# A one-core hybrid block: two unread products in the opening, gate Silus, rotary keys and column sums issued later

## The chip, the core and the metric

The kernel runs on one core of a Trainium2 chip. Its metric is the device time of one execution in microseconds (us), lower is better. The core has five engines with a queue each: TensorE (PE in the profile, with its weight loads as PEld), VectorE (DVE), ScalarE (ACT), GpSimd (POOL) and SyncE (SP, which only issues transfers here). Each engine takes its instructions in the order in which the program was laid out for it, and waits on semaphores for the others.

## The reference, cut to what matters

One layer of a streaming encoder on 512 tokens of width 1024, all in float32. The three parts read and add to the same `x`:

```python
mod = silu(c) @ w_ada + b_ada                  # nine vectors of 1024
h = rms(x) * (1 + s1) + sh1
x = x + 0.5 * g1 * swiglu(h, ffn1_w_in, ffn1_w_out)
h = rms(x) * (1 + s2) + sh2
x = x + g2 * hybrid_mixer(h)                   # two groups of four heads, then w_out
h = rms(x) * (1 + s3) + sh3
x = x + 0.5 * g3 * swiglu(h, ffn2_w_in, ffn2_w_out)
```

The mixer multiplies `h` by `w_in` and splits the result. Group A is a gated delta rule: convolutions and Silu on q, k and v, a chunked recurrence, then `rms(o) * silu(z)` with a gate `z` of its own. Group B is latent attention: low-rank q and kv lifted by two small matrices, norms of each head, rotary positions on 64 columns of every q head and on one key `kr` that all heads share, block-causal softmax, a norm of each head's output. Both groups are put side by side and multiplied by `w_out`.

## The kernel before

Activations stand with features on the 128 partitions and tokens along the row: `xT` is eight tiles of 128x512. A float32 product is written as three products of a reduced type: weights and activations are each split in a high part (a cast on ACT, `wh`, `hh`, `ah`, `mh`) and a low part (a subtraction on DVE, `wl`, `hl`, `al`, `ml`), and `mm3` issues high x high, high x low and low x high (lines 267 to 269). Small products (transposes against the identity, attention, the delta rule) stay in plain float32.

**Stages.** `phase0` (0 to about 62 us) transposes the tokens, works out the first modulation and the first six products of FFN1 while weights stream in. FFN1 goes on to about 330 us, its second matrix (`down`) to about 403 us, the mixer from there to about 692 us, and FFN2 to the end.

**What sets the order.** `phase0` and the body of FFN2 are laid out by hand: under `in_order` every instruction follows the one written before it on its engine. `down`, `first_units` and the delta recurrence keep only their products in written order. The rest of the mixer is written as generators (`Side`) that are stepped by turns between groups of large products; a scheduler then fixes one order for each engine. An activation from another table than the one loaded makes ACT load a table (`ACT_TABLE_LOAD`, 1.28 us); the method `table` therefore chains all Exp and Silu activations in the order in which they are written, through `self.tabled`.

The places that the change touches:

- **Opening** (`phase0`, lines 313 to 330). TensorE turns the token tiles `xt` (line 316). ACT sums their squares (line 321), POOL takes a power for the norm (line 179), DVE scales the first 128 columns (`xn`, line 348). TensorE then makes the columns of the modulation from `ar`, a slice of `w_ada` (line 415), turns `xn` (line 357), sums four partial rows (line 335), turns the last token tile, and waits for the first high part `hh` (line 362, ACT) to make six products of it (line 375); line 442 spreads the norm over the partitions.
- **Column sums at the seams** (`norm_half`, `first_units`). The token norm at the end of a part is worked out by halves. While the first products of the next part run on half 0, `first_units` steps the norm of half 1 at numbered marks: the first step is the column sum (`colsum`, line 536, which needs DVE's or POOL's last addition to `na`, line 478) with what follows it on POOL and DVE (the power and the diagonal `dg`), the second spreads it (line 442), the third modulates. The marks stand at line 735 for FFN2 (`(7, 18, 15)`, the products of two units by turns) and at line 1246 for the mixer (`(6, 15, 14)`, one unit).
- **Rotary key** (`prep_k`, lines 1843 to 1881). The key after its rotation is `kro` (DVE, lines 1889 to 1893 and 1859); four transposes (line 1869) and a copy (line 1871) make `krT`, which each attention block reads at line 1908. Behind it the step goes on with the other key columns, `kn`: squares, a power in nine steps on DVE, a scaling by head, transposes and a scaled copy `nT` (`head_tiles`, lines 1783 and 1785).
- **Gate Silus** (`mixer`, line 2048). When the last of four large gate products is laid out, four Silus of `z` are issued. The attention blocks (`attend`) of the second pair of heads still run then: their Exp, transposes (line 1925), value products (line 1935), copies out (`ao`, line 1948; `hn`, line 1939), and at the end `attended`, which scales (`on`), turns (line 1966) and splits (`mh`, line 1971; `ml`, line 1972) a head. Beside them four inversions of 128x128 blocks run (`inverse`, lines 1573 to 1616, `join`, lines 1636 to 1646). The gate is read only in `gated_out` (line 1760).

Of the kernel before, what the change touches and what calls it, by code (L numbers as in the profile page):

```python
# [14 lines left out]
AF = mybir.ActivationFunctionType  # L15
# [3 lines left out]
P = 128  # L19
# [3 lines left out]
NB = NT // P  # L23
# [56 lines left out]
class Block:  # L80
# [216 lines left out]
    def phase0(self):  # L297

        nc = self.nc
# [13 lines left out]
        def raw(b, j):  # L313
            pt = self.aux()
            for t in range(4):
                nc.tensor.transpose(pt[:, t * P:(t + 1) * P], self.xtok[b][j][:, t * P:(t + 1) * P], self.ident)
            nc.vector.tensor_copy(xall[:, 4 * j:4 * j + 4, b * P:(b + 1) * P], pt.rearrange("p (t c) -> p t c", t=4))
# [8 lines left out]
        r = self.rms_cols(v, NB, D)  # L326
        for i in (4, 5, 6):
            raw(*tiles[i])
        self.c1, self.c2 = self.const([P, KT], s="sh"), self.const([P, KT], s="s1")
        self.new_h()  # L330

# [23 lines left out]
        pt = self.aux()  # L355
# [376 lines left out]

    def ffn2(self, nb):
        with self.tc.tile_pool(name="ws", bufs=1) as self.ws:
            ps = self.first_units(3, nb, 2, (7, 18, 15))
            with self.in_order():
                self.ffn2_rest(ps)

# [500 lines left out]
    def latents(self, nb):  # L1239

        nc = self.nc
        wq = self.up_weight("mla_w_uq", self.vcol["mla_q_norm_w"], 3, 384)
        wkv = self.up_weight("mla_w_ukv", self.vcol["mla_kv_norm_w"], 2, 512)
        next(wq)
        next(wkv)
        ps = self.first_units(3, nb, 1, (6, 15, 14))

        def gather(ps):
            parts, acc = [], None
            for p in ps:  # L1250
                parts.append(self.split(p, "lat"))
                sq = self.slot(s="lsq")
                nc.scalar.activation(sq, p, AF.Square)
                if acc is None:
                    acc = sq
                else:
                    nc.vector.tensor_tensor(out=acc, in0=acc, in1=sq, op=ALU.add)
            return parts, acc

        pk = self.proj(self.aux())  # L1260
        qp, acc = gather(ps)
        ps = [pk]
        lq = qp, self.rms_cols(self.colsum(acc), NB, 384)
        p = self.proj()
        s = self.slot(s="kab")
        nc.scalar.copy(s[:72, :], p[:72, :])
        wq = next(wq)
        ps.append(self.proj())
        kp, acc = gather(ps)
        lkv = kp, self.rms_cols(self.colsum(acc), NB, 256)  # L1270
        wkv = next(wkv)
        return lq, wq, lkv, wkv, s
# [569 lines left out]
    def prep_k(self, kn):  # L1842

        nc = self.nc
        sk_n = self.const([P, 16], s="skn")
        kr = self.kab[:, :288].rearrange("p (b c) -> p b c", b=NB)[:, :, :64]
        s = self.slot(s="krq")
        sv = s[:, :256].rearrange("p (b c) -> p b c", b=NB)
        nc.scalar.activation(sv, kr, AF.Square)
        ss = self.small(4, "krs")  # L1850
        nc.vector.tensor_reduce(out=ss, in_=sv, axis=AX.X, op=ALU.add)
        rr = self.rms_cols(ss, 4, 64)
        kx = self.slot(s="krx")
        xv = kx[:, :256].rearrange("p (b c) -> p b c", b=NB)
        self.mul(xv, kr, self.bc(rr, 4, 64))
        ko = self.slot(s="kro")
        ov = ko.rearrange("p (b e c) -> p b e c", b=NB, e=2)
        self.rope(ov[:, :, 0, :], xv, self.rope_c["k"], self.rope_s["k"])
        nc.vector.tensor_copy(ov[:, :, 1, :], ov[:, :, 0, :])
        yield  # L1860
        for b in range(NB):
            s = self.slot(s="akk")
            nc.scalar.activation(s, kn[b], AF.Square)
            nc.vector.tensor_reduce(out=sk_n[:, 4 * b:4 * b + 4], in_=s.rearrange("p (h d) -> p h d", h=4), axis=AX.X,
                                    op=ALU.add)
        rkn = self.rms_cols(sk_n, 16, 128)
        pt = self.aux()
        for b in range(NB):
            nc.tensor.transpose(pt[:, b * P:(b + 1) * P], ko[:, b * P:(b + 1) * P], self.ident)
        self.krT = self.slot(s="krT")  # L1870
        nc.scalar.copy(self.krT, pt)
        yield
        for b in range(NB):
            kv = kn[b].rearrange("p (h d) -> p h d", h=4)
            self.mul(kv, kv, self.bc(rkn[:, 4 * b:4 * b + 4], 4))
        yield
        jk = self.vcol["qkn_k_nope"]
        for h in range(4):
            self.knT.append(self.head_tiles([kn[b][:, h * P:(h + 1) * P] for b in range(NB)], self.cwT[:, jk:jk + 1]))
            yield  # L1880

    def rope(self, out, x, c, s):
# [76 lines left out]
    def attended(self, h, r):  # L1959


        nc = self.nc
        on = self.head_scale(self.ao[h], r)
        pt = self.aux()
        for i in range(NB):
            nc.tensor.transpose(pt[:, i * P:(i + 1) * P], on[:, i * P:(i + 1) * P], self.ident)
        yield
        j = self.vcol["mla_out_norm_w"]
        gain = self.cwT[:, j:j + 1]
        mh, ml = self.mixed[4 + h] = self.slot(F32R, "mh"), self.slot(F32R, "ml")  # L1970
        nc.scalar.activation(mh, pt, AF.Copy, scale=gain)
        nc.vector.scalar_tensor_tensor(out=ml, in0=pt, scalar=gain, in1=mh.bitcast(F32), op0=ALU.mult, op1=ALU.subtract)


    def mixer(self, nb):
        nc, tc = self.nc, self.tc
# [19 lines left out]
        def silu(tiles):  # L1996
            for t in tiles:
                self.table(t, t, AF.Silu)
# [46 lines left out]

        chain.add(solving())
        self.dense_units(4, Rates(sides, (1, 0.75, 2)), 1, z_done)
        silu(self.zT)
        accum = self.slot(s="na")

        fill = Side()
# [1 line left out]
        def others():  # L2053
            while att.open or att.todo:
                att.step()
                yield
            fill.add(self.out_attended())

        rest = Side(wide=3)
        rest.add(others())  # L2060
        while self.wk[1] is None or deltas.open or deltas.todo:
            chain.step(2)
# [112 lines left out]
```

## Time and profile before

| | us |
|---|---|
| median of 3 runs | 1050.69 |
| the 3 runs | 1050.64, 1050.69, 1052.29 |
| the profiled execution, its own time | 1052.1 |
| its span in the profile | 1050.4 |
| PE busy | 1032.6 |
| DVE busy | 682.1 |
| ACT busy | 449.0 |
| POOL busy | 48.2 |

The span is the stretch that the profile's clock covers; the execution's own time has 1.7 us around it. Lines of the profile name an engine, a line of the kernel, an operation and its tiles as out<-in. In the order of time, a row gives start, length, engine, line, and in square brackets how long the engine was idle before and what released it. In the chain that ended last, a row gives start, share of the chain, engine and line. A row of waits gives the total, the count and the longest. A row of stretches gives the busy time of each engine with the number of instructions, the granted share of TensorE's clock (PEclk) and what the DMA engines did.

### The profile page before, as it was taken

What the parts mean: (1) busy time and instruction counts of PE and PEld (TensorE: products, weight loads), DVE (VectorE), ACT (ScalarE), POOL (GpSimd) and SP (SyncE); (2) the same over time, 40 slices, a digit from 0 to 9 for tenths busy, and PEclk for the clock granted to TensorE, in tenths of its full rate; (3) what the DMA queues carried; (4) which work ended last, traced back from release to release, by engine and by line L of the source; (5) the groups of instructions that cost most, each with busy time, mean ns of one, the idle gap of its engine ahead of it and who ended that gap; (6) DMA issues with size and microseconds to landing.
All of it is one profiled execution on the core that took longest, in us unless ns stands there. A gap on an engine that the chain in (4) does not pass through costs nothing.

```text
span 1050.4 us, 16101 instructions
## 1 busy us (share of the span) xinstructions
PE 1032.6 (98%) x6375; PEld 884.5 (84%) x6375; DVE 682.1 (65%) x1251; ACT 449.0 (43%) x781; POOL 48.2 (5%) x113
## 2 busy tenths in 40 slices
PE   6999999999999999999999999999999999999998
PEld 5788878788887799887777769998999999999986
DVE  4478984333486636648877556789768778777633
ACT  3342322222222226739566464465345444444422
POOL 1000000000000011100001111310000000000000
PEclk8999999999999999999999999999999999999999
DMA  9979973233586539711212201173423333333222
GB/s 275 288 224 301 303 237 101 85 96 95 184 279 220 164 99 236 179 41 51 70 42 55 72 22 41 41 162 100 136 78 102 108 101 112 92 98 105 76 61 81
DMA packets 203689, 136.88 MB, mean 130 GB/s; under 512 B 13777, under 2 KB 186590, under 8 KB 203614
## 3 DMA queue, kind: packets, MB, share of 16 engines
q1 hardware_dynamic: 202318, 131.14, 42.4%
q0 software_dynamic: 1296, 4.72, 2.4%
q8 instruction: 50, 0.82, 0.3%
q14 instruction: 25, 0.20, 0.1%
HBM read 128.63 MB, written 2.49 MB: 125 GB/s over the span
## 4 chain that ended last, share of the span: by engine, by line
PE 89%; ACT 4%; DVE 3%; DMA 1%; issue 1%; POOL 0%; SPq 0%; POOLq 0%; DVEq 0%; ACTq 0%
PE pa L267 20%; PE pa L268 20%; PE pa L269 19%; PE pb L870 6%; PE pb L869 6%; PE pb L871 6%; PE pb L268 1%; PE pb L267 1%; PE pb L269 1%; PE pb L415 1%; PE pb L1491 1%; PE pb L1905 1%; DMA xt<-in_x 1%; PE pb L1908 1%; PE pb L1935 0%
## 5 line engine op out<-in xcount | busy, mean ns | idle before, releaser
L267 PE MATMUL pa<-hh,wh 128*128 128x512 f32 (+1 forms) x565 | 216.7, 384 | 0.0
L268 PE MATMUL pa<-hl,wh 128*128 128x512 f32 (+1 forms) x565 | 214.8, 380 | 0.6 <-DVE hl L454 0.4
L269 PE MATMUL pa<-hh,wl 128*128 128x512 f32 (+1 forms) x565 | 214.6, 380 | 0.0
L193 ACT CAST wh<-wr 128x1024 fp32r<-128x1024 f32 (+1 forms) x106 | 107.8, 1018 | 247.7 <-PE pa L268 172.0
L198 DVE TENSOR_TENSOR wl<-wr,wh 128x1024 fp32r<-128x1024 f32 (+1 forms) x97 | 114.2, 1178 | 104.6 <-ACT wh L193 102.2
L267 PE MATMUL pa<-ah,wh 128*128 128x512 f32 (+1 forms) x396 | 145.6, 368 | 0.6 <-DVE xT L896 0.4
L268 PE MATMUL pa<-al,wh 128*128 128x512 f32 (+1 forms) x396 | 144.5, 365 | 0.0
L269 PE MATMUL pa<-ah,wl 128*128 128x512 f32 (+1 forms) x396 | 143.6, 363 | 0.0
L267 PEld LDWEIGHTS pa<-hh,wh 128*128 128x128 f32 x565 | 106.4, 188 | 23.1 <-issue 3.2
L269 PEld LDWEIGHTS pa<-hh,wl 128*128 128x128 f32 x565 | 106.3, 188 | 20.5 <-issue 0.9
L268 PEld LDWEIGHTS pa<-hl,wh 128*128 128x128 f32 x565 | 106.5, 188 | 19.4 <-DVE hl L454 1.0
L269 PEld LDWEIGHTS pa<-ah,wl 128*128 128x128 f32 x396 | 74.8, 189 | 12.1
L267 PEld LDWEIGHTS pa<-ah,wh 128*128 128x128 f32 x396 | 75.2, 190 | 10.3 <-ACT wh L193 1.7
L268 PEld LDWEIGHTS pa<-al,wh 128*128 128x128 f32 x396 | 75.2, 190 | 7.2
L574 DVE SCALAR_TENSOR_TENSOR aa<-ar,sc,aa 128x512 f32<-128x512 f32 x98 | 72.9, 747 | 9.5 <-DMA ar<-in_w_ada 8.3
L896 DVE SCALAR_TENSOR_TENSOR xT<-pa,mod,xT 128x512 f32<-128x512 f32 (+1 forms) x40 | 29.3, 735 | 17.6 <-PE pa L269 17.6
L869 PE MATMUL pb<-fh,wh 128*128 128x256 f32 x144 | 40.7, 283 | 0.0
L871 PE MATMUL pb<-fh,wl 128*128 128x256 f32 x144 | 40.7, 283 | 0.0
L871 PE MATMUL pb<-hh,wl 128*128 128x256 f32 x144 | 40.7, 283 | 0.0
L870 PE MATMUL pb<-fl,wh 128*128 128x256 f32 x144 | 40.7, 282 | 0.0
L870 PE MATMUL pb<-hl,wh 128*128 128x256 f32 x144 | 40.7, 282 | 0.0
L869 PE MATMUL pb<-hh,wh 128*128 128x256 f32 x144 | 40.6, 282 | 0.0
(443 smaller groups left out, 2008.4 us busy)
## 6 DMA issues: line engine op xcount, KB each, us to landing
wr<-in_ffn_w_in SPq DMA_DIRECT2D x82, 512.0 KB, 3.9
ar<-in_w_ada SPq DMA_DIRECT2D x48, 512.0 KB, 6.0
wr<-in_ffn_w_out SPq DMA_DIRECT2D x34, 512.0 KB, 3.7
ar<-in_w_ada SPq DMA_DIRECT2D x48, 256.0 KB, 4.9
wr<-in_w_in SPq DMA_DIRECT2D x21, 512.0 KB, 3.7
wr<-in_ffn_w_out SPq DMA_DIRECT2D x17, 384.0 KB, 3.4
wl<-wr POOLq DMA_DIRECT2D x9, 512.0 KB, 6.0
wr<-in_w_out SPq DMA_DIRECT2D x8, 512.0 KB, 3.7
```

The lines of the kernel that those rows point to most:

```text
L193: self.nc.scalar.copy(hi, raw)
L198: self.nc.vector.tensor_tensor(out=lo, in0=raw, in1=hi.bitcast(F32), op=ALU.subtract)
L267: mm(out, wh, xh, start=start, stop=False)
L268: mm(out, wh, xl, start=False, stop=False)
L269: mm(out, wl, xh, start=False, stop=stop)
L415: nc.tensor.matmul(pg[32 * q:32 * q + 32, :256], self.sc[:, kc:kc + 1].to_broadcast([P, 32]), a[:, kc], start=(e == 0), stop=(e == 1), til ...
L574: nc.vector.scalar_tensor_tensor(out=acc, in0=a, scalar=sc, in1=acc, op0=ALU.mult, op1=ALU.add)
L869: mm(out, wh, xh, start=start and k == 0, stop=False, **kw)
L870: mm(out, wh, xl, start=False, stop=False, **kw)
L871: mm(out, wl, xh, start=False, stop=stop and k == 3, **kw)
L896: nc.vector.scalar_tensor_tensor(out=self.xT[t][:, ts], in0=p[:, ts], scalar=gate[:, t:t + 1], in1=self.xT[t][:, ts], op0=ALU.mult, op1=AL ...
L1491: nc.tensor.matmul(pa[:, ps], kh[:, ps], x[:, ps], start=True, stop=True)
```

## The change

- In `phase0`, behind the transposes of seven token tiles, TensorE makes the same float32 product of the identity and a token tile twice, into a PSUM tile that nothing reads.
- The first mark of `first_units` goes from 7 to 8 for FFN2 and from 6 to 7 for the mixer.
- The transposes of the rotary key and the copy `krT` go from ahead of the scaling of `kn` to behind the second of four `head_tiles`.
- The Silus of the gate go from the end of the gate's products to the end of the attention blocks; the chain of table activations is first moved on to the last `mh` (`self.ended`), so that the Silus stay behind it on ACT.

```diff
@@ phase0
         for i in (4, 5, 6):
             raw(*tiles[i])
+        unread = self.aux()
+        for _ in range(2):
+            nc.tensor.matmul(unread, self.ident, self.xtok[0][0], start=True, stop=True)
         self.c1, self.c2 = self.const([P, KT], s="sh"), self.const([P, KT], s="s1")
@@ ffn2
-            ps = self.first_units(3, nb, 2, (7, 18, 15))
+            ps = self.first_units(3, nb, 2, (8, 18, 15))
@@ latents
-        ps = self.first_units(3, nb, 1, (6, 15, 14))
+        ps = self.first_units(3, nb, 1, (7, 15, 14))
@@ prep_k
         rkn = self.rms_cols(sk_n, 16, 128)
-        pt = self.aux()
-        for b in range(NB):
-            nc.tensor.transpose(pt[:, b * P:(b + 1) * P], ko[:, b * P:(b + 1) * P], self.ident)
-        self.krT = self.slot(s="krT")
-        nc.scalar.copy(self.krT, pt)
         yield
...
             self.knT.append(self.head_tiles([kn[b][:, h * P:(h + 1) * P] for b in range(NB)], self.cwT[:, jk:jk + 1]))
+            if h == 1:
+                pt = self.aux()
+                for b in range(NB):
+                    nc.tensor.transpose(pt[:, b * P:(b + 1) * P], ko[:, b * P:(b + 1) * P], self.ident)
+                self.krT = self.slot(s="krT")
+                nc.scalar.copy(self.krT, pt)
             yield
@@ attended
-        nc.scalar.activation(mh, pt, AF.Copy, scale=gain)
+        self.ended = nc.scalar.activation(mh, pt, AF.Copy, scale=gain).ins.name
@@ mixer
         self.dense_units(4, Rates(sides, (1, 0.75, 2)), 1, z_done)
-        silu(self.zT)
         accum = self.slot(s="na")
...
                 att.step()
                 yield
+            self.tabled = self.ended
+            silu(self.zT)
             fill.add(self.out_attended())
```

**TensorE in the opening.** Ahead of the modulation's columns stood the last transposes of token tiles (`xt`; `ident` is the identity, `sg` the partial rows, `xn` the scaled first columns). Before:

```order
L316 MATMUL pb_182<-ident_92,xt_81 128x128 x4
L316 MATMUL pb_188<-ident_92,xt_82 128x128 x4
L415 MATMUL pb_222<-ar_108,sc_124 32x256 x8
L357 MATMUL pb_234<-ident_92,xn_212 128x128 x4
L335 MATMUL pb_222<-sel_128,sg_231 128x1 x2
```

With the change:

```order
L316 MATMUL pb_182<-ident_92,xt_81 128x128 x4
L316 MATMUL pb_188<-ident_92,xt_82 128x128 x4
L331 MATMUL pb_194<-xt_76,ident_92 128x512 x2
L418 MATMUL pb_225<-ar_108,sc_124 32x256 x8
L360 MATMUL pb_237<-ident_92,xn_215 128x128 x4
L338 MATMUL pb_225<-sel_128,sg_234 128x1 x2
```

The two unread products stand between the transposes and the columns; nothing else moves there.

**TensorE in the mixer, at the rotary key.** Among the large products for the convolutions (`pa`, from `hh` and `hl` and the split weights `wh`, `wl`) the four transposes of the key `kro` stood alone. Before:

```order
L267 MATMUL pa_4531<-hh_3172,wh_4380 128x512
L1869 MATMUL pb_4461<-ident_92,kro_4426 128x128 x4
L268 MATMUL pa_4531<-hl_3173,wh_4380 128x512
L269 MATMUL pa_4531<-hh_3172,wl_4381 128x512
L267 MATMUL pa_4641<-hh_3158,wh_4526 128x512
```

With the change:

```order
L267 MATMUL pa_4866<-hh_3163,wh_4739 128x512
L1786 MATMUL pb_4502<-ident_92,kn_4042 128x128
L1786 MATMUL pb_4509<-ident_92,kn_4042 128x128
L1881 MATMUL pb_4516<-ident_92,kro_4429 128x128 x3
L1786 MATMUL pb_4502<-ident_92,kn_4043 128x128
L1786 MATMUL pb_4509<-ident_92,kn_4043 128x128
L1881 MATMUL pb_4516<-ident_92,kro_4429 128x128
```

The transposes of `kro` moved behind some fifty more large products, into the run of the sixteen transposes of `kn`, which had stood together at nearly the same place before.

**ScalarE at the end of attention.** Rows with `z` and L168 are the gate's Silus; `ao`, `hn` and `mh` belong to the last heads of attention, `U`, `ti` and `T` to the inversions, whose products TensorE makes between large ones. Before:

```order
L1929 COPY pT_5580<-pb_5575 128x512
L168 ACT_TABLE_LOAD
L168 ACTIVATE z_5288<-z_5288 128x512
L1948 COPY ao_5086<-pb_5582 128x128
L1586 COPY U_5613<-ti_5391 32x4x32 x2
L1598 COPY ti_5244<-pb_5638 32x128 x2
L1988 COPY z_5748<-pa_5679 128x512
L168 ACTIVATE z_5490<-z_5490 128x512
L1939 ACTIVATE hn_5623<-pb_5582 128x256
L1948 COPY ao_5088<-pb_5582 128x128
L168 ACTIVATE z_5671<-z_5671 128x512
L168 ACTIVATE z_5748<-z_5748 128x512
```

With the change the copies of the last heads follow `pT` at once, and behind the last `mh` there stands:

```order
L1975 ACTIVATE mh_5670<-pb_5661,cwT_811 128x512
L1601 COPY ti_5343<-pb_5706 32x128 x2
L1601 COPY ti_5394<-pb_5723 32x128 x2
L168 ACT_TABLE_LOAD
L168 ACTIVATE z_5291<-z_5291 128x512
L168 ACTIVATE z_5493<-z_5493 128x512
L168 ACTIVATE z_5674<-z_5674 128x512
L168 ACTIVATE z_5751<-z_5751 128x512
L1619 COPY T_5802<-pb_5801 64x256
```

The table load and the four Silus moved from ahead of `ao` and `hn` to a place between the last `ti` and the first copy `T` of the inversions. The number of table loads in the program is the same.

On TensorE the laying out of this stretch changed with it: the eight value products (L1935) of the last pair come ahead of the inversions' next products, and of the ten large products that stood right ahead of the last transposes of `on` (L1966) eight others (`pa` from `hh`, for the gate) stand there now, the ten behind. The column sums (L536) at both seams stand three large products later than before. VectorE and GpSimd take a few neighbouring instructions of these stretches in another order; SyncE's order is the same.

## The prediction

> **What bounds the kernel now.** I read the page first: how busy TensorE is, its clock by slices, and the shares of the chain that ended last.
>
> ```profile
> PE 1032.6 (98%) x6375; PEld 884.5 (84%) x6375; DVE 682.1 (65%) x1251; ACT 449.0 (43%) x781; POOL 48.2 (5%) x113
> PEclk8999999999999999999999999999999999999999
> PE 89%; ACT 4%; DVE 3%; DMA 1%; issue 1%; POOL 0%; SPq 0%; POOLq 0%; DVEq 0%; ACTq 0%
> ```
>
> The reader is to see that TensorE is the bound nearly everywhere, and that one slice alone, the first, has less than the full clock. The change takes no product away and adds two. It can save time only where TensorE waits or runs slowly. So I looked next at TensorE's waits, the longest first.
>
> ```profile
> PE pb L305 <- DMA vecs<-in_b_ada: 3.0, 1, 3.0
> PE pb L316 <- DMA xt<-in_x: 2.9, 1, 2.9
> PE pb L415 <- DVE xn L348: 1.9, 1, 1.9
> PE pb L1966 <- DVE on L1229: 1.5, 1, 1.5
> PE pb L1869 <- DVE kro L1859: 0.8, 1, 0.8
> ...
> PE pb L536 <- DVE na L478: 0.5, 2, 0.3
> ```
>
> The first two rows are the start's transfers, which the change leaves alone. The four others are its four places: 4.7 us together. Then I cut the opening into stretches at the moments where the granted clock changes, and set two stretches of the mixer beside them, which hold the 1.5 us wait.
>
> ```profile
> core 0: us, PE busy (x) PEld busy (x) DVE busy (x) ACT busy (x) POOL busy (x), PEclk, DMA share, GB/s
> 12.33:15.74 3.41, 1.46 (x19) 0.83 (x19) 2.89 (x11) 0.12 (x1) 0.73 (x1) 1.00 1.16 316
> 15.74:19.16 3.42, 3.14 (x14) 2.59 (x13) 2.35 (x6) 1.79 (x3) 0.14 (x5) 0.50 1.17 310
> 19.16:22.57 3.41, 3.41 (x7) 1.71 (x6) 1.27 (x2) 0.00 (x0) 0.98 (x30) 0.50 1.21 297
> 22.57:25.98 3.41, 3.41 (x29) 2.38 (x29) 0.54 (x3) 0.96 (x2) 0.00 (x0) 1.00 1.16 314
> ...
> 613.06:616.47 3.41, 2.74 (x14) 1.96 (x13) 0.58 (x2) 3.35 (x9) 0.70 (x1) 1.00 0.00 0
> 616.47:619.88 3.41, 2.55 (x60) 2.10 (x60) 3.09 (x4) 2.11 (x6) 0.00 (x0) 1.00 0.02 5
> ```
>
> This is the view that decides. The clock is 1.00 from 12.33, falls to 0.50 at 15.74, and comes back at 22.57: two stretches of 3.41 us at half pace. The stretch ahead of the fall had TensorE busy for 1.46 of 3.41 us (43%). The two mixer stretches had it busy for 80% and 75%, and the clock stayed.
>
> **The change part by part.** The sum is made against the profiled execution's own time, 1052.1 us.
>
> *The unread products.* Where they go and what they could spare:
>
> ```profile
> 6.30 6.20 PE L316 MATMUL pb<-ident,xt 128*128 128x128 f32 x28 [2.91 <-DMA xt<-in_x]
> ...
> 15.54 0.86 PE pb L357 x4
> ...
> 17.43 0.82 ACT hh L362
> 18.29 1.65 PE pa L375 x3
> 19.94 1.28 PE pb L375 x3
> 21.22 1.59 PE pb L442 x2
> ...
> 602.09 1.72 PE pb L1905 x4
> ```
>
> (The first row is from the order of time, the others from the chain that ended last.) The transposes end at 6.30 + 6.20 = 12.50, and line 415 waits 1.9 us more. Two float32 products of 128x512 at full clock cost 1.72 us: the last row holds two such products, written as four passes. They fit into the pause, so in themselves they cost nothing: xn on DVE hides them. Without that cover, or at half clock (line 442: 1.59 us for one such product, so 3.2 us), up to 1.3 us would come on the path.
>
> With them the stretch from 12.33 has TensorE busy for 1.46 + 1.72 = 3.18 of 3.41 us, 93%, above the 75% at which the clock stayed. If it stays here too, the chain's work between 15.74 and 22.57 runs at full pace: of line 357 0.66 us lie behind 15.74 (it ends at 16.40), line 375 has 1.65 + 1.28, line 442 has 22.57 - 21.22 = 1.35, together 4.94 us, of which half goes: 2.47. Line 335, beside these, halves too. I take **-2.5**. The bounds: 2.9 if line 335's half (it releases hh through a vector operation) comes on top; and 0 if the clock falls all the same. Transfers may take some of it: the DMA share in these stretches is above 1, so the queues are full, and weights needed 2.5 us sooner don't land sooner. I count up to 0.4 for it in the range.
>
> *Column sums.* At the seam into the mixer and at the one into FFN2:
>
> ```profile
> 405.67 0.14 issue
> 405.81 0.57 PE pb L536 x4
> ...
> 694.32 0.61 PE L536 MATMUL pb<-ones,na 128*128 128x1 f32 x4 [0.33 <-DVE na L478]
> ...
> 695.58 0.39 PE L268 MATMUL pa<-hl,wh 128*128 128x256 f32 x1 [0.42 <-DVE hl L454]
> ```
>
> The first two rows are of the chain, the last two of the order of time. Three products of 128x256 (each shorter than the 0.39 us of such a row) now stand ahead of each sum, about as much as the waits. In the mixer's seam the wait goes: the waits' row gives both as 0.5, so 0.17 beside FFN2's 0.33, with 0.14 of issue: **-0.3**. In FFN2 TensorE waits 0.42 us for hl soon after. What it no longer waits for at line 536 it waits for there, because the vector and scalar chain to hl isn't shortened: **0**. The other end for both: -0.6; and +0.4 if the norm of half 1, which now starts three products later, becomes late.
>
> *Rotary key.* The rows in the order of time:
>
> ```profile
> 508.51 0.63 PE L1869 MATMUL pb<-ident,kro 128*128 128x128 f32 x4 [0.79 <-DVE kro L1859]
> ...
> 520.00 2.50 DVE L1229 TENSOR_TENSOR kn<-kn,ry 128x512 f32<-128x512 f32 x4
> ...
> 523.17 2.42 ACT L1785 ACTIVATE nT<-pb,cwT 128x512 f32<-128x512 f32 x4 [1.21 <-PE pb L1783]
> ...
> 524.33 0.48 PE L1908 MATMUL pb<-krT,qrT 64*128 64x128 f32 x2
> ```
>
> The idle 0.79 us goes, since kro is 12 us old where the transposes stand now. The transposes themselves cost the same there. The copy krT now queues on ACT among the four copies nT (2.42 / 4 = 0.6 us each), which end only at 525.6, while line 1908 reads krT from 524.33. It stands behind the second nT, so it lands at about 523.17 + 3 x 0.6 = 525.0, but the transposes of kn also come out earlier by the 0.79 us: late by nearly nothing. What is late next is kn itself (520.00), which VectorE sets; TensorE has large products until then. I take **-0.8**, between -1.1 (switches between small and large products saved too) and 0 (all of it met again at line 1908, since the two later nT now wait 0.6 us behind krT).
>
> *Gate Silus.* Again in the order of time:
>
> ```profile
> 610.19 1.28 ACT L168 ACT_TABLE_LOAD   x1
> 611.49 0.63 ACT L168 ACTIVATE z<-z 128x512 f32<-128x512 f32 x1
> ...
> 614.61 0.36 ACT L1939 ACTIVATE hn<-pb 128x256 f32<-128x256 f32 x1
> ...
> 616.50 1.29 DVE L1229 TENSOR_TENSOR on<-ao,roots 128x512 f32<-128x512 f32 x2 [0.88 <-POOL roots L179]
> 617.33 0.63 PE L1966 MATMUL pb<-ident,on 128*128 128x128 f32 x4 [1.53 <-DVE on L1229]
> ...
> 622.46 0.37 ACT L1616 COPY T<-pb 64x256 f32<-64x256 f32 x1 [1.07 <-PE pb L1615]
> ...
> 625.33 0.79 PE L1636 MATMUL pb<-T,at 64*64 64x64 f32 x10
> ```
>
> Table load and Silus, 1.28 + 4 x 0.63 = 3.8 us, stand ahead of hn, and hn leads through a power on POOL to on, for which TensorE waits 1.53 us. Before, TensorE could turn on 617.33 - 614.61 = 2.7 us after hn began. In the new order hn needs only the value products, which end near 610.9, and two copies U ahead of it: it begins near 611.3, so line 1966 can start near 614.0. TensorE gets there near 613.3, since eight large products still lie ahead of it, and the ten that covered it before lie behind. That leaves some 0.7 us of wait at line 1966 and 0.2 at line 1935, which now reads pT right behind its copy: 1.53 - 0.9 = **-0.6**. Bounds: -1.5 (no new wait) and 0 (the same wait as before). What is queued behind the Silus now is the copies T. The Silus start behind the last ti; in the new order TensorE has fifteen large products and 4 us of small ones between there and line 1636, against some 5 us on ACT for ti, Silus and T. That hides them; without the cover the first T would be late by up to 3.8 us.
>
> The sum: 1052.1 - 2.5 - 0.3 - 0.8 - 0.6 = **1047.9 us**. The median before is 1.4 us below the profiled execution. If the unprofiled runs lost less to the clock in the opening, part of the 2.5 us isn't there to be won, and 1047.9 stands as the floor that both have; if the 1.4 lie elsewhere, the median falls to 1046.5.
>
> **The rivals.**
>
> *The mixer gives its gains back* (line 1908 waits for krT, line 1966 for on). For it: both places end in chains of scalar and vector work that the change reorders but hardly shortens. Against it: TensorE is 89% of the chain, so these chains seldom end last. Time: 1052.1 - 2.5 - 0.3 = 1049.3.
>
> *The clock falls all the same.* In the stretch 15.74 to 19.16 TensorE waits for hh in any case; at full pace its 3.14 us shrink, while the products of line 375 move in, and I estimate 2.4 of 3.42 us busy, 70%, just under the 75% seen to be kept. If that drops the clock at 19.16, one stretch of half pace stays and half of 3.41 us is lost again: 1052.1 - 0.8 - 1.7 = 1049.6. If it falls at 15.74 as now, the opening gives nothing: 1052.1 - 1.7 = 1050.4. For it: at 92% busy (3.14 of 3.42) the half clock was kept at 19.16, so busy time alone doesn't explain the grant. Against it: 43% against 93% is a wide step. The Trainium skill, "TensorE: Matmul & The Clock Gate" (Part 1: The HAM clock gate), has the clock fall only after about 3.4 us of idleness; a pause of 1.9 us would then not be the cause, and the sum would be 1050.4. The row 12.33 to 15.74 speaks against that: 1.46 us of work in it, and the clock fell. Its Part 4 (PE-mode transpose) says that transposes don't count as busy in the same way; no row here shows that apart, and it would favour a later fall, as there are transposes in the stretch from 15.74.
>
> *Slower.* The copies T come late: they stand behind 3.8 us of table and Silus on ACT. If the last ti, which waits for TensorE's small products, comes so late that 2 us of this are uncovered, TensorE idles for 2 us at line 1636, more than the 1.9 us ahead of the clock's fall in the opening, and then two stretches at half pace cost up to 3.4 us more: 1052.1 - 3.6 + 2 + 3.4 = 1053.9. It decides from about 1.7 us of uncovered wait (half of a stretch). Against it: my count above leaves ACT 1 us or more to spare.
>
> **How the numbers follow.** Chances: the forecast 0.50, the mixer's gains given back 0.21, the clock falls all the same 0.22, slower 0.07. A measurement of this kernel tells 0.2% (2.1 us) from no change: faster is below 1048.6, slower above 1052.8. The forecast lies below that bound but for its upper edge, which the two lesser rivals reach down to if the unprofiled 1.4 us count: faster 0.53, same 0.40, slower 0.07. The range: 1045.8 (the median's 1046.5 with the larger opening or key) to 1050.5 (the unchanged clock's 1050.4).
>
> **What would show it.** Right: the granted clock 1.00 in all stretches from 12.33 on, the products inside the pause with line 415 still near 14.45, line 375's six products in about 1.5 us, line 415's second round near 20.2; no wait at line 536 in the mixer's seam and none at the transposes of kro, and at most 0.9 us around lines 1935 and 1966. Wrong: 0.50 in any stretch before 25; a wait for krT at line 1908, for T at line 1636, or for ar at line 415.

## The result, and the profile after

The changed kernel takes 1047.53 us in the median (1047.19 to 1048.07, 6 runs), the kernel before 1051.5 us (1050.64 to 1052.29, 6 runs): a ratio of 0.9967, 95% interval 0.9956 to 0.9978. The profiled execution took 1047.25 us, with a span of 1045.6 us against 1050.4. On another chip, as run e10_after below, the medians were 1047.78 us (12 runs) and 1051.29 us (29 runs), a ratio of 0.9956 (0.9938 to 0.9973).

The page of the changed kernel: engine time and TensorE's clock.

```profile
PE 1029.0 (98%) x6379; PEld 882.2 (84%) x6379; DVE 682.6 (65%) x1251; ACT 448.6 (43%) x781; POOL 48.2 (5%) x113
...
PEclk9999999999999999999999999999999999999999
```

There are four more matmul records (the two unread products, two passes each), and still 3.6 us less of TensorE time: 2.4 us less up to the products that stood at 60 us, where work ran at half clock before, and 0.9 us less in the mixer from 500 to 700 us. The first slice now has the full clock.

TensorE's waits in the changed kernel, total, count and longest:

```profile
PE pb L418 <- DVE xn L351: 1.4, 1, 1.4
PE pb L1939 <- ACT ao L1952: 0.9, 2, 0.4
PE pa L378 <- ACT hh L365: 0.8, 1, 0.8
...
PE pa L267 <- ACT hh L465: 0.4, 1, 0.4
...
PE pb L1786 <- DVE kn L1232: 0.4, 1, 0.4
...
PE pb L1970 <- DVE on L1232: 0.4, 1, 0.4
...
PE pa L268 <- DVE hl L457: 0.3, 1, 0.3
```

The waits for kro and na are gone, and that for on fell from 1.5 to 0.4. New ones stand beside them: for kn 0.4, a second one of 0.4 for the copies of attention, and for hh 0.4 at the seam into FFN2; in the opening the wait for hh at line 378 is 0.8 where it was 0.3, since TensorE arrives sooner at full clock. Each edit passed a part of its wait on.

The opening in stretches of the granted clock (stretch, its length, TensorE busy with the number of instructions, granted clock, then the DMA), and the products in order of time:

```profile
9.71:13.12 3.41, 3.41 (x20) 1.00 1.17 318
13.12:16.54 3.42, 2.03 (x25) 1.00 1.16 315
16.54:19.95 3.41, 2.66 (x14) 1.00 1.16 315
19.95:23.36 3.41, 3.41 (x28) 1.00 1.16 298
...
11.26 1.88 PE L331 MATMUL pb<-xt,ident 128*128 128x512 f32 x4
14.53 1.09 PE L418 MATMUL pb<-ar,sc 128*32 128x256 f32 x16 [1.39 <-DVE xn L351]
17.98 0.96 PE L378 MATMUL pa<-hh,wh 128*128 128x512 f32 x3 [0.75 <-ACT hh L365]
18.78 0.85 PE L378 MATMUL pb<-hh,wh 128*128 128x512 f32 x3
...
20.42 1.09 PE L418 MATMUL pb<-ar,sc 128*32 128x256 f32 x16
```

The unread products lie in the pause, line 418 (415 before) still starts near 14.5, and the clock stays at 1.00.

To see where the 4.8 us of span went, I matched TensorE's instructions of the two traces by code line and tiles and took the difference of their starts:

| place | start, after minus before (us) |
|---|---|
| second round of modulation columns, 22.7 us | -2.3 |
| after 58 us | -2.1 |
| after the seam into the mixer, 406 us | -2.5 |
| last scores of attention, 604 us (2332 large products done in both) | -4.5 |
| first output product of the delta rule, 665 us (2433 done in both) | -4.8 |
| end of the FFN2 products | -4.9 |

So between these places the trace gained 2.1 us (opening), 0.35 (column sums), 2.0 (key) and 0.3 (end of attention). The kernels below show which of this holds in every execution.

### The profile page after: what moved, and what is told of

The parts are those of the page before. It is cut to its first block, busy times and chain, and to the rows that moved or that the text cites. A ratio compares the mean times of both kernels' runs of the same rounds, so it can differ in the third digit from the quotient of the medians.

```text
span 1045.6 us, 16109 instructions
## 1 busy us (share of the span) xinstructions
PE 1029.0 (98%) x6379; PEld 882.2 (84%) x6379; DVE 682.6 (65%) x1251; ACT 448.6 (43%) x781; POOL 48.2 (5%) x113
## 4 chain that ended last, share of the span: by engine, by line
PE 90%; ACT 4%; DVE 4%; issue 1%; DMA 1%; POOL 0%; SPq 0%; POOLq 0%; ACTq 0%; DVEq 0%
PE pa L267 20%; PE pa L268 20%; PE pa L269 20%; PE pb L872 6%; PE pb L873 6%; PE pb L874 6%; PE pb L267 1%; PE pb L268 1%; PE pb L269 1%; PE pb L1909 1%; PE pb L418 1%; PE pb L1939 1%; PE pb L1494 1%; DVE cv L1438 1%; PE pb L1912 1%
```

## The experiments

Beside the time, each execution lists the mean granted clock. That turned out to be the key to these runs: two half-clock stretches of 3.41 us cost 3.41 / 1050, so they show as 0.997, and a single one as 0.998. (Behind the last products of the program the clock falls as well; in the traces that takes up to 0.001 off. An execution with 0.999 or more thus had no other fall.)

**Each edit alone.** e1_products puts only this into the kernel before:

```diff
+        unread = self.aux()
+        for _ in range(2):
+            nc.tensor.matmul(unread, self.ident, self.xtok[0][0], start=True, stop=True)
```

> The kernel before with the two unread products alone. Theory A (the pause lets the clock fall, the products keep it): the granted clock is 1.00 in every stretch from 12.3 us on, the second round of modulation columns starts near 20.4 us instead of 22.7, and the time is 2.0 to 2.4 us below the kernel before. Rival B (the clock in the opening depends on where the free-running stretches fall, not on the products): the clock still falls to 0.50 in some profile, and the time is within 0.5 us of the kernel before. Rival C (they help, but weights land later than needed): 20.4 us as in A, but less than 1.5 us is left at 60 us.

Measured: 1050.22 us (11 runs) against 1051.12 (31 runs), ratio 0.9994 (0.9980 to 1.0008). In the two profiles the second round of columns starts 2.4 us earlier, as A says, but the executions tell more. Of the kernel before, 89 executions in three jobs list their clock: 44 at 0.999 or more, median 1050.24 us, and 45 below, median 1052.35. With the products, ten of eleven show 0.999 or more, median 1050.14; the eleventh shows 0.991 at 1057.9. The products thus remove the fall of the clock, which half of the executions of the kernel before have, and give nothing to the other half. Rival B is right in so far that chance decides, A in that the products take the chance away.

C's number holds too, though weights are not the cause: by 58 us, 1.2 of the 2.4 us are lost again. VectorE in order of time, in the kernel before:

```profile
53.89 0.15 DVE L337 SCALAR_TENSOR_TENSOR s<-pb,vT 128x1 f32<-128x1 f32 x1
53.96 0.16 DVE L1363 COPY ex<-vb 128x4 f32<-128x4 f32 x1
54.08 0.75 DVE L460 SCALAR_TENSOR_TENSOR hm<-xT,s,rb 128x512 f32<-128x512 f32 x1
```

and in e1_products:

```profile
51.53 0.15 DVE L340 SCALAR_TENSOR_TENSOR s<-pb,vT 128x1 f32<-128x1 f32 x1
54.06 0.17 DVE L1366 COPY ex<-vb 128x4 f32<-128x4 f32 x1 [2.38 <-DMA vb<-in_gdn_a_log]
54.14 0.75 DVE L463 SCALAR_TENSOR_TENSOR hm<-xT,s,rb 128x512 f32<-128x512 f32 x1
```

A copy of four columns that is read in the mixer's gates, at 460 us, was scheduled here. In e1_products its vector has not landed, VectorE stands for 2.38 us, and behind it waits hm, on which the next products of FFN1 hang: TensorE then waits 0.56 us for hh and 0.28 for hl. In the kernel before this copy ran at 53.96 us and nobody waited.

e2_key moves only the transposes of the rotary key and their copy, as the change does.

> The kernel before with the rotary key's transposes and copy moved, nothing else. Theory A (the move pays twice: 0.5 us at the key's transposes and some 1.4 us between 548 and 570 us, where the attention of the first heads is ordered in another way): 1.6 to 2.1 us below the kernel before. Rival (only the wait for the key goes; the gain after 548 us belongs to the Silus' move): 0.3 to 0.8 us below.

Measured: 1048.26 us (7 runs), ratio 0.9970 (0.9958 to 0.9981); the four executions at 0.999 or more have a median of 1047.92, against 1050.48 for the 15 such executions of the kernel before in the same job: 2.6 us less. By the traces, at the last scores of attention (2332 large products done in both), it starts 1.10 us earlier though its opening was 0.35 later: 1.45 us. The rival is out. Of theory A's 1.6 to 2.1 us the traces give a little less and the executions more; why they differ by 1.1 us is open (four executions are few, and each of the two traces is of one execution). Theory A's places do not hold. In e2_key three more large products are done by 541 us, 3 x 0.23 = 0.7 us, so the start there, 0.2 us earlier, hides that nearly all of the gain is made by then: 0.2 + 0.35 + 0.7 = 1.2. What seemed a gain after 548 us was those products having moved ahead. TensorE in order of time, before:

```profile
507.32 0.39 PE L267 MATMUL pa<-hh,wh 128*128 128x512 f32 x1
508.51 0.63 PE L1869 MATMUL pb<-ident,kro 128*128 128x128 f32 x4 [0.79 <-DVE kro L1859]
508.89 0.47 PE L268 MATMUL pa<-hl,wh 128*128 128x512 f32 x1
```

and in e2_key:

```profile
520.71 0.44 PE L1783 MATMUL pb<-ident,kn 128*128 128x128 f32 x2 [0.42 <-DVE kn L1229]
520.98 0.49 PE L1878 MATMUL pb<-ident,kro 128*128 128x128 f32 x3
521.31 0.43 PE L1783 MATMUL pb<-ident,kn 128*128 128x128 f32 x2
521.58 0.27 PE L1878 MATMUL pb<-ident,kro 128*128 128x128 f32 x1
521.69 1.59 PE L1783 MATMUL pb<-ident,kn 128*128 128x128 f32 x12
```

Standing alone, the four transposes took 508.89 - 507.32 - 0.23 = 1.34 us of TensorE's time, of which 0.79 was the wait. Within the run they take 0.33 + 0.11 = 0.44 (by the starts). That is 0.9; the other 0.3 and the 0.25 up to 604 us lie in other groupings and in a wait of 0.15 us that went, against 0.42 of new wait for kn. They were not taken apart.

e3_silus moves only the gate's Silus.

> The kernel before with the gate's Silus moved to the end of attention, nothing else. Theory A: TensorE's wait of 1.5 us ahead of line 1966's transposes shrinks to 0.4, a wait of 0.4 for the copies pT or ao appears, and 0.3 to 0.6 us are left at the end. Rival (the gain between 548 and 570 us belongs to this move): 1.6 to 2.0 us below the kernel before. Second rival (the first inversions' copies T are late): no gain.

Measured: 1050.28 us (11 runs), ratio 0.9993 (0.9984 to 1.0003): the median can't tell it. Its profiled execution kept the clock without products, so only differences within the mixer count: -1.52 us up to 566 us, -1.30 at 568, -1.35 at the last scores, -1.64 at 665 us. The end of attention gains 0.3, but 0.2 were lost ahead of it, and 0.1 is left. TensorE's waits in e3_silus:

```profile
PE pb L1935 <- ACT ao L1948: 0.9, 2, 0.4
...
PE pb L1966 <- DVE on L1229: 0.4, 1, 0.4
...
PE pb L1966 <- DVE bt L1546: 0.3, 1, 0.3
```

The wait for on shrank by 1.1, a second one of 0.4 appeared at line 1935: 0.7 fewer, of which 0.3 arrive. The wait for bt is new; it stands at 566 us, ahead of the first heads' transposes at line 1966, and takes the 0.2. T is never waited for. The waits are theory A's; what is left at the end, 0.1 us in this trace, is below its 0.3 to 0.6.

e4_marks moves only the two marks.

> The kernel before with the two first marks moved by one product unit (8 for 7 and 7 for 6), nothing else. Theory A: 0.35 us below, all of it at 404 us, none at 694 us. Rival (the wait moves to the later products there too): 0.0 us.

Measured: 1050.75 us (12 runs), ratio 0.9993 (0.9975 to 1.0011), again too little for the median. (The executions at 0.999 or more have medians of 1049.71 in e3_silus, of seven, and 1049.70 in e4_marks, of six, against 1050.48: 0.8 us less in both, more than the traces show, but within the spread of so few.) In the trace, its lag of 0.39 us from the opening is 0.02 after 406 us: a gain of 0.37, which is theory A. At 694 us nothing changes, as the wait takes another place. TensorE in order of time, e4_marks:

```profile
694.37 0.38 PE L267 MATMUL pa<-hh,wh 128*128 128x256 f32 x1 [0.38 <-ACT hh L462]
...
695.10 0.39 PE L268 MATMUL pa<-hl,wh 128*128 128x256 f32 x1 [0.34 <-DVE hl L454]
...
695.44 0.50 PE L536 MATMUL pb<-ones,na 128*128 128x1 f32 x4
```

**What keeps the clock.** e5_no_products takes the products out of the changed kernel.

> The changed kernel without the two unread products. Theory A (the products only keep the clock from falling, which it does in about half of the executions): the executions in which the mean granted clock stays at 0.999 or more take as long as the changed kernel, about 1047.5 us; others, some half of them, show 0.995 to 0.998 and take 1 to 3 us more; the median is 0.5 to 1.5 us above the changed kernel. Rival (the products pay 2.3 us in every execution, as the two profiles say): all executions about 1049.8 us.

Measured: 1049.31 us (11 runs, 1047.28 to 1052.17). Four executions show 0.999 or more, median 1048.15, seven less, median 1050.27. This is theory A. (Not each of the seven need have lost the clock in the pause: the one that was profiled lost it at 58 us, as shown below.) e6_transposes, on the same chip, has transposes in their place:

```diff
-        for _ in range(2):
-            nc.tensor.matmul(unread, self.ident, self.xtok[0][0], start=True, stop=True)
+        for k in range(14):
+            nc.tensor.transpose(unread[:, k % 4 * P:k % 4 * P + P], self.xtok[0][0][:, k % 4 * P:k % 4 * P + P], self.ident)
```

> The changed kernel with fourteen more unread 128x128 transposes of the same token tile in place of the two unread products, about as long (14 x 0.13 = 1.9 us). Theory A (what counts is that TensorE is busy): all executions but strays keep a mean clock of 0.999 or more, and the median is that of the changed kernel, 1047.5 us. Rival (transposes don't count as busy): half of the executions show 0.995 to 0.998, as without products, and the median is 0.5 to 1.5 us higher.

Measured: 1047.97 us (1047.27 to 1048.95), all eleven at 0.999 or more. Transposes count as busy. The rival, which is what the Trainium skill says in "TensorE: Matmul & The Clock Gate" (Part 4: PE-mode transpose), does not hold for these transposes. e7_one_product has `range(1)`.

> The changed kernel with one unread product instead of two. Theory A (the clock falls after a free-running stretch of 3.41 us in which TensorE was busy for less than about 1.5 us; without products the worst stretches seen had 0.93 to 1.46): one product adds 0.86 us, so the worst stretch has 1.8 us, the clock never falls, and the median equals that of the changed kernel beside it. Rival (both products are needed, since the stretch has to be nearly full): a part of the executions shows 0.995 to 0.998, and the median is 0.3 us or more higher.

Measured: 1047.86 us, all twelve at 0.999 or more, beside 1047.78 for the changed kernel. One product is enough.

The stretches explain it. In each trace the clock changes on a grid of 3.41 us whose place differs from execution to execution (it came on between 9.71 and 12.33 us). So each trace is cut on its own grid here, in the columns used above. (The 0.93 in the last expectation is of e5_no_products, cut on the grid of the kernel before; on its own, that trace's lowest stretch in the opening has 1.68 us, and its clock stayed.) e2_key:

```profile
12.21:15.62 3.41, 0.98 (x18) 1.00 1.16 315
15.62:19.04 3.42, 3.22 (x20) 0.50 1.17 308
```

e4_marks:

```profile
11.99:15.40 3.41, 1.18 (x17) 1.00 1.16 315
15.40:18.82 3.42, 3.42 (x24) 0.50 1.18 305
```

e3_silus:

```profile
12.22:15.63 3.41, 1.73 (x23) 1.00 1.16 316
15.63:19.05 3.42, 2.67 (x17) 1.00 1.17 309
```

e9_copy_alone (below), which has no products either:

```profile
9.97:13.38 3.41, 1.51 (x14) 1.00 1.17 317
13.38:16.80 3.42, 2.00 (x24) 1.00 1.16 316
```

With the 1.46 us of the kernel before (stretch 12.33 to 15.74), the clock fell after stretches with 0.98, 1.18 and 1.46 us of work, and stayed after 1.51 and 1.73. So a pause of 2 us costs the clock only where the grid puts most of it into one stretch. e5_no_products shows the same far from the opening, at the small copy's place, where that execution's TensorE waited 1.9 us for hh:

```profile
55.13:58.54 3.41, 1.21 (x10) 1.00 0.76 222
58.54:61.95 3.41, 3.41 (x11) 0.50 0.95 319
61.95:65.36 3.41, 3.41 (x16) 1.00 0.74 237
```

The edge is not sharp, though. In the same trace, at the program's end, the clock fell after a stretch with 1.65 us, more than the 1.51 after which it stayed in e9_copy_alone:

```profile
1044.99:1048.40 3.41, 1.65 (x13) 1.00 0.41 119
1048.40:1050.47 2.07, 0.00 (x0) 0.50 0.20 57
```

**The small copy.** e8_late_copy and e11_late_copy (the same kernel on two chips) hold the copy back in the changed kernel, e9_copy_alone in the kernel before:

```diff
-        v.tensor_scalar(out=t4(eb), in0=kv[:, :, 68:72], scalar1=-1.0, scalar2=None, op0=ALU.mult)
-        v.tensor_copy(ea, self.alog)
+        late = v.tensor_scalar(out=t4(eb), in0=kv[:, :, 68:72], scalar1=-1.0, scalar2=None, op0=ALU.mult)
+        self.follow(v.tensor_copy(ea, self.alog).ins, late.ins.name)
```

e8_late_copy:

> The changed kernel with one small copy on VectorE (line 1366, 128x4, from a vector that lands at 53 to 54 us), which stood ahead of the modulation of a later row of FFN1 at 53 us, held back to the gates of the mixer at 460 us, where it is read. Theory A (this copy waits for its transfer and so gives back up to 1.2 of the 2.3 us that the opening wins): 0.2 to 1.1 us below the changed kernel, no wait for hh at 55 us, and less spread between executions. Rival (the weights' transfers set the pace there anyway): within 0.2 us of the changed kernel, with the wait at another line before 65 us.

e9_copy_alone:

> The kernel before with that small copy held back, nothing else. Theory A: executions that keep the clock win up to 1.1 us (to about 1049.2 us), those whose clock falls win nothing, since their TensorE comes 2.3 us later anyway; the median is 0.2 to 0.8 us below the kernel before. Rival (the copy isn't the cap): no gain, 1051 us.

e10_after, the changed kernel itself:

> The changed kernel once more, as what the two others of this job are compared with on one chip: 1047.5 us, all executions at a mean clock of 0.999 or more.

e11_late_copy:

> The changed kernel with the small copy of line 1366 held back, beside the changed kernel on one chip. Theory A (the copy caps the opening's gain in part of the executions): 0.2 to 0.6 us below the changed kernel in the median. Rival (the 0.3 us seen between two chips was the chips): within 0.1 us.

Measured: e8_late_copy 1047.63 us (7 runs), not below the 1047.53 of the changed kernel on another chip, so its size can't be read there. e9_copy_alone 1050.37 us, ratio 0.9998 (0.9982 to 1.0013): its six executions at 0.999 or more have a median of 1049.38, 0.7 us below those of the kernel before in the same job (1050.12), its five others 1051.9; theory A's sizes, though the ratio can't tell them from nothing. On one chip, e11_late_copy has 1047.34 us and the changed kernel (e10_after) 1047.78: 0.44 us less, with nine of twelve executions below 1047.5 against three of twelve. The spreads overlap, so that the size is uncertain, and one execution of e11_late_copy lost the clock (0.996, 1050.02 us) in spite of the products; where is not known. That the wait goes is in the trace. VectorE in order of time, e8_late_copy:

```profile
52.06 0.15 DVE L340 SCALAR_TENSOR_TENSOR s<-pb,vT 128x1 f32<-128x1 f32 x1
52.24 0.75 DVE L463 SCALAR_TENSOR_TENSOR hm<-xT,s,rb 128x512 f32<-128x512 f32 x1
```

Now hm follows s at once, and TensorE waits for nothing between 20 and 70 us. e11_late_copy has the lowest median of all: ratio 0.9948 (0.9928 to 0.9967) to the kernel before; against the changed kernel it is ahead by less than the spread.

## Why the prediction was right, step by step

The forecast was 1047.9 us; the median is 1047.53, the profiled execution 1047.25. Signs and places were right, three sizes were not, and the errors partly cancel: the key gave more than its term, the opening and the Silus less. The terms add up to 4.2 us, the two profiled executions are 4.85 apart, the medians 4.0. That the number came within 0.4 us is therefore in part luck.

- **Opening, -2.5.** The traces gave 2.3 us at 22 us and 2.1 after 58. The prediction's signs are there: line 418 near 14.5, the six products in 1.5 us, the second round at 20.42. The mechanism is shown: with products or transposes in the pause (e1, e6, e7, e8, e10, e11), 63 of 65 executions kept 0.999 or more; of the 141 without (e2, e3, e4, e5, e9 and the 89 before), 71 did. Two steps failed. The 93% took the stretches to lie where they lay before; in the changed kernel's trace they lay 2.6 us earlier, and the least busy one had 59%. That was enough, but it is not the stretch that was worked out. The other is the step from one profile to all executions. The term was worked out from an execution in which the clock fell, as it does in half of them; the others had no half-clock work to lose. The prediction's sentence on the median (1047.9 as a floor for both) allowed for this and is what happened: against executions that keep the clock the change brings some 2.6 us (1050.24 to about 1047.6), against the others 4.7.
- **The rival "the clock falls all the same"** named 70% busy as a risk. The trace of the changed kernel kept the clock after stretches with 2.03 and 2.66 us of work, 59% and 78%, and the edge lies at about 1.5 to 1.65 us, 44% to 48%. The rule of idleness for a whole stretch that the prediction weighed is refuted by the falls after 0.98 to 1.46 us of work.
- **Transfers in the opening** were expected to take up to 0.4. They took 0.2 in the changed kernel's profile and 1.2 in that of e1_products, by a small vector rather than by weights. A wait for ar, named as a sign of being wrong, did come in e1_products (1.49 us ahead of line 418), but it ended at 14.50, no later than the wait for xn in the changed kernel (14.53).
- **Column sums, -0.3 and 0.** 0.35 and 0.37 in two traces at the mixer; nothing at FFN2, where the wait went to hh and hl, as was said.
- **Rotary key, -0.8.** Mis-sized: 1.45 us in e2_key, 2.0 in the changed kernel, above the bound of 1.1. The term held only the wait of 0.79. A lone group of four transposes among large products cost 0.55 us beside its wait, against 0.44 within a run of its like, and later groupings gave some more. The wait that the prediction saw coming, at line 1908, did not come; one of 0.4 came for kn, and the gains above are net of it. The 0.55 us by which the changed kernel gains more than e2_key lie between 558 and 569 us. At 566.6 us e2_key waits 0.24 for bt ahead of line 1967's transposes, as e3_silus does; the changed kernel does not. That is a part; the rest is open, as is why the executions of e2_key gain more than its trace.
- **Gate Silus, -0.6.** The waits behaved as forecast: 0.4 at on and 0.4 at line 1935's successor, 0.8 together against 0.9 (the row of 0.9 for ao counts an older wait near 550 us too). But only 0.3 us arrive at 665 us, and the Silus' move alone kept 0.1; where the rest went was not taken apart. The slower case did not come near. Table and Silus ended at 617.57, the first T lasted to about 617.97 (0.37 us each), and line 1639, which reads it, started at 619.24 without a wait:

```profile
614.08 1.28 ACT L168 ACT_TABLE_LOAD   x1
615.38 2.19 ACT L168 ACTIVATE z<-z 128x512 f32<-128x512 f32 x4
617.60 1.18 ACT L1619 COPY T<-pb 64x256 f32<-64x256 f32 x4
```

(ScalarE in order of time, the changed kernel. The cover left over is 1.3 us; the prediction counted 1 or more.)

## What to carry to other kernels

Before a stall is costed, ask how many executions have it: the mean granted clock of each execution showed at once what one profile could not. Where TensorE pauses for some 2 us, a little unread work that fits into the pause can hold the clock (one product of 0.86 us was enough here); it is worth nothing where the clock wouldn't have fallen. Count what has moved ahead of a point before a start that came earlier or later there is taken for a gain or a loss.

## What the runs showed of the hardware

- The clock's grid of 3.41 us lies anywhere relative to the program. I cut all thirteen traces on their own grids, from the first full clock almost to the end. Four stretches had less than 1.5 us of TensorE work (0.98, 1.18, 1.21, 1.46), and after each of them the clock fell; after every other stretch, with 1.51 us or more, it stayed. At the program's very end it falls too, in nine traces after stretches with 0 to 1.45 us, but in e5_no_products after one with 1.65. So the edge lies at about 1.5 to 1.65 us, and busy time as the traces give it doesn't fix it alone.
- In the opening it stayed at half for two stretches, in e4_marks although the first had TensorE busy throughout (3.42 of 3.42 us, transposes and small products among them). At 58.54 us, with large products and four of one column, it came back after one. Why, no run tells.
- Eight of the 89 executions of the kernel before show a mean clock of 0.988 to 0.991 and take 1056.6 to 1059.2 us, and single ones of e1_products and e4_marks do so too. None of them was profiled, so where their clock is lost stays open.
